# RMSNorm with a matmul on one core: two of the output stores divided by rows

## The chip, the core and the metric

The kernel runs on one core of a Trainium2 chip. The metric is the device time of one launch in microseconds, the median of several runs. A profile of one further run shows what every engine did: TensorE (PE, with weight loads as PEld), VectorE (DVE), ScalarE (ACT), GpSimd (POOL), SyncE (SP), and the DMA engines that move data between HBM and the on-chip buffer.

## What is computed

```python
def setup_inputs():
    batch, seq, dim, out_dim = 16, 1024, 512, 768
    return {
        "x": np.random.randn(batch, seq, dim).astype(np.float32),
        "gamma": np.ones(dim, dtype=np.float32),
        "weight": np.random.randn(dim, out_dim).astype(np.float32) * 0.1,
        "eps": np.float32(1e-5),
    }

def reference(x, gamma, weight, eps):
    rms = np.sqrt(np.mean(x ** 2, axis=-1, keepdims=True) + eps)
    x_norm = x / rms * gamma
    return np.matmul(x_norm, weight).astype(np.float32)
```

There are 16 × 1024 = 16,384 tokens. x has 512 and the output 768 float32 values for each, so 33.6 MB come in and 50.3 MB go out, and 1.6 MB of weights come in once.

## The kernel before

The tokens are handled as 128 tiles of 128 tokens. Each tile is cast to bf16, transposed (by TensorE, for some tiles by VectorE), multiplied with the weights, and scaled by 1/rms on its way from PSUM to an output buffer. ScalarE and VectorE take turns at that last step.

Transfers cover several tiles. The tokens of a group of 16 tiles lie so over the partitions that each partition holds 16 consecutive tokens; a store of 8 tiles is thus 128 rows of 8 × 768 × 4 = 24,576 consecutive bytes.

```python
XG, OG = 16, 8          # tiles of an input and of an output group
last = NT // OG - 1
x_first, x_size = stretches(XG, {0: [2, 2, 4, 8], **{g: [8, 8] for g in range(1, NT // XG)}})
o_first, o_size = stretches(OG, {0: [2, 2, 4], 1: [4, 4], last - 1: [4, 4], last: [4, 2, 2]})

def rows(ap, i, n):
    base, t = (x_first[i], x_size[i]) if i < XG else (i - i % XG, XG)
    return ap[base * P:(base + t) * P, :].rearrange("(p t) d -> p t d", t=t)[:, i - base:i - base + n, :]
...
xt = [sb(f"xt{n}", [P, XG, D], F32) for n in range(2)]     # two input buffers of 16 tiles
ot = [sb(f"ot{n}", [P, OG, O], F32) for n in range(3)]     # three output buffers of 8 tiles
```

The scaled tile goes into one of the three `ot` buffers. When the last tile of a stretch is in, SyncE issues the store of the stretch:

```python
def store(i):
    first, n = o_first[i], o_size[i]
    s = first // OG % 3
    if i == first + n - 1:
        src = ot[s][:, first % OG:first % OG + n, :]
        order.transfer(SP, lambda: SP.dma_start(out=rows(out, first, n), in_=src), reads=cells("ot", s, first % OG, n))
...
def finish_tile(i, a, engine):
    s = i // OG % 3
    before = [("ot", s, i % OG - 1)] if i == o_first[i] + o_size[i] - 1 else []
    scale(engine, ot[s][:, i % OG, :], ops[a][:, :O], rstd[:, i:i + 1],
          [("ops", a, 0), ("ops", a, 1), ("rstd", i)] + before, [("ot", s, i % OG)])
    store(i)
```

`order` keeps all instructions with the buffer cells that they read and write, and from these sets the semaphore waits: a tile is written into `ot` again only when the store that reads its former content has landed. The PSUM accumulators (`ops`) are three as well. The loads of x stand in the same SyncE queue as the stores:

```python
def load_until(i):
    while starts and starts[0] < i:
        load(starts.pop(0))
...
for j in range(1, NP):                       # pairs of tiles
    load_until((2 * j + AHEAD + XG - 1) // XG * XG)
    ...
    for i, engine in ((2 * j, ACT), (2 * j + 1, DVE)):
        a = accumulator()
        matmuls(i, a, range(K), feed)
        finish_tile(i, a, engine)
```

Of the kernel before, what the change touches and what calls it, by code (L numbers as in the profile page):

```python
# [16 lines left out]
P = 128  # L17
# [83 lines left out]
def kernel(  # L101
# [9 lines left out]
    PE, DVE, ACT, POOL, SP = nc.tensor, nc.vector, nc.scalar, nc.gpsimd, nc.sync  # L111
    order = Order(tc)
# [5 lines left out]
    out = out.flatten_outer_dims()  # L118
# [5 lines left out]
    XG, OG = 16, 8  # L124
    AHEAD = 20

    def stretches(group, parts):
        first, size, i = {}, {}, 0
        for g in range(NT // group):
            for n in parts.get(g, [group]):  # L130
                for t in range(i, i + n):
                    first[t], size[t] = i, n
                i += n
        return first, size

    last = NT // OG - 1
    x_first, x_size = stretches(XG, {0: [2, 2, 4, 8], **{g: [8, 8] for g in range(1, NT // XG)}})
    o_first, o_size = stretches(OG, {0: [2, 2, 4], 1: [4, 4], last - 1: [4, 4], last: [4, 2, 2]})

    def rows(ap, i, n):  # L140
        base, t = (x_first[i], x_size[i]) if i < XG else (i - i % XG, XG)
        return ap[base * P:(base + t) * P, :].rearrange("(p t) d -> p t d", t=t)[:, i - base:i - base + n, :]

    def sb(name, shape, dtype):
        return nc.alloc_sbuf_tensor(name, shape, dtype).ap()
# [14 lines left out]
    ot = [sb(f"ot{n}", [P, OG, O], F32) for n in range(3)]  # L160
# [7 lines left out]
    def cells(name, slot, i, n=1):  # L168
        return [(name, slot, t) for t in range(i, i + n)]
# [117 lines left out]
    def store(i):  # L287
        first, n = o_first[i], o_size[i]
        s = first // OG % 3
        if i == first + n - 1:  # L290
            src = ot[s][:, first % OG:first % OG + n, :]
            order.transfer(SP, lambda: SP.dma_start(out=rows(out, first, n), in_=src), reads=cells("ot", s, first % OG, n))

    def hold(lhsT, cell):
        run(PE, lambda: PE.ldweights(lhsT), [cell])  # L295
# [20 lines left out]
# [7 lines that stand above are left out]
# [157 lines left out]
```

## Time and profile before

| what | value |
|---|---|
| time, median of 3 runs | 209.54 us (209.4 to 209.75) |
| span of the profiled run | 207.7 us, granted TensorE clock 0.986 |
| DMA packets | 6064, 85.62 MB |
| stores of 8 tiles | 12, each 3072 KB, median 17.8 us from issue to landing |
| loads of 8 tiles | 15, each 2048 KB, median 21.6 us from issue to landing |
| store of tiles 40 to 47 | issued at 82.61 us, landed at 103.64 us |
| store of tiles 72 to 79 | issued at 129.45 us, landed at 153.15 us |

The span counts from the first to the last instruction of the core. The profile gives the busy time of each engine, a row of digits in which each stands for the busy tenths of one fortieth of the span, and the waits: engine and line, the thing waited for, microseconds in total, how many times, the longest. The DMA row is the mean over 16 DMA engines. A transfer from SyncE is divided over these engines, and it has landed when the last of its completion events is in.

### The profile page before, as it was taken

To read this page: it belongs to the slowest core of one execution; us is meant where nothing else is said; L and a number is where in the kernel's file an instruction comes from. 1 tells how busy PE (TensorE), PEld (TensorE's weight loads), DVE (VectorE), ACT (ScalarE), POOL (GpSimd) and SP (SyncE) were. 2 spreads that over 40 slices of the span, in tenths; PEclk is the share of its full clock that TensorE was granted. 3 is DMA by queue.
4 is the path that set the end of the run, shared out by engine and by line. 5 is a ranking of instruction groups with operands and counts; after the bars stand their busy time and mean duration, and the time that the engine had idled before them with its cause. 6 is when DMAs were issued, how large, how long until landed. Compare 5 with 4: busy or idle time off the path is not lost.

```text
span 207.7 us, 2772 instructions
## 1 busy us (share of the span) xinstructions
PE 193.6 (93%) x1212; PEld 72.9 (35%) x717; DVE 149.4 (72%) x255; ACT 144.5 (70%) x343; POOL 60.0 (29%) x34
## 2 busy tenths in 40 slices
PE   7889999999999999999999999999999999999900
PEld 1234444433344334333443333343434334433300
DVE  0455647998589957998589966998589966999310
ACT  4698897877768686877768686868778397863300
POOL 3147652047202740055200660006700175000000
PEclk9999999999999999999999999999999999999995
DMA  6999999999999999999999999999999999999992
GB/s 237 421 443 426 353 393 428 436 432 427 443 410 429 437 439 420 429 417 434 439 420 424 421 451 429 410 429 420 439 426 418 431 443 434 431 431 407 431 399 103
DMA packets 6064, 85.62 MB, mean 412 GB/s; under 512 B 674, under 2 KB 676, under 8 KB 1700
## 3 DMA queue, kind: packets, MB, share of 16 engines
q1 hardware_dynamic: 6048, 85.46, 97.4%
q8 instruction: 7, 0.11, 0.2%
q14 instruction: 5, 0.04, 0.0%
q10 hardware_dynamic: 4, 0.00, 0.0%
HBM read 35.13 MB, written 50.33 MB: 411 GB/s over the span
## 4 chain that ended last, share of the span: by engine, by line
PE 88%; DMA 4%; issue 1%; SPq 1%; POOL 1%; DVE 0%
PE ps L299 78%; PE ps L229 10%; DMA xt<-in_x_dram 4%; POOL xb L187 1%; DVE ot L280 0%; SPq L344 0%; SPq L176 0%; SPq L475 0%; SPq L434 0%
## 5 line engine op out<-in xcount | busy, mean ns | idle before, releaser
L299 PE MATMUL ps<-w_bf,xT 128*128 128x256 bf16 (+1 forms) x783 | 145.0, 325 | 1.3 <-DVE w_bf L280 0.2
L278 ACT ACTIVATE ot<-ps,rstd 128x768 f32<-128x768 f32 x64 | 57.5, 898 | 44.2 <-PE ps L299 39.6
L195 ACT ACTIVATE jk<-xt 128x512 bf16<-128x512 f32 x128 | 78.8, 619 | 5.0 <-DMA xt<-in_x_dram 4.9
L187 POOL CAST xb<-xt 128x2048 bf16<-128x2048 f32 (+3 forms) x21 | 46.4, 2218 | 113.0 <-DMA xt<-in_x_dram 110.1
L280 DVE TENSOR_SCALAR ot<-ps,rstd 128x768 f32<-128x768 f32 x64 | 64.8, 1013 | 8.6 <-PE ps L299 7.9
L295 PEld LDWEIGHTS <-xT 128*128 128x128 bf16 x400 | 39.3, 98 | 59.4 <-issue 51.5
L229 PE MATMUL ps<-ident_f,xb 128*128 128x128 f32 x200 | 54.4, 277 | 0.9 <-POOL xb L187 0.9
L238 DVE COPY xT<-ps 128x1024 bf16<-128x1024 bf16 (+1 forms) x53 | 34.6, 653 | 24.8 <-PE ps L229 23.1
L270 DVE STREAM_TRANSPOSE xTq<-xq 32x256 f32<-32x256 f32 x112 | 48.8, 435 | 3.4
L229 PEld LDWEIGHTS ps<-ident_f,xb 128*128 128x128 f32 x200 | 28.5, 143 | 46.3 <-issue 42.9
L299 PE MATMUL ps<-w_bf,xTq 128*128 128x256 bf16 (+1 forms) x217 | 41.8, 324 | 0.4
L195 ACT ACTIVATION_READ_ACCUMULATOR jk<-xt 128x1 f32 x128 | 24.4, 190 | 0.0
L295 PEld LDWEIGHTS <-xTq 128*128 128x128 bf16 x112 | 10.9, 98 | 14.5 <-issue 14.5
L259 POOL CAST xq<-xt 128x2048 bf16<-128x2048 f32 x7 | 13.2, 1893 | 0.0
L202 DVE RECIPROCAL rstd<-rms 128x8 f32<-128x8 f32 (+3 forms) x20 | 3.9, 193 | 7.4 <-ACT rms L200 7.2
L200 ACT ACTIVATE rms<-ssq,eps_sb 128x8 f32<-128x8 f32 (+3 forms) x20 | 6.0, 300 | 0.7
L299 PE MATMUL ps<-warm 128*128 128x512 bf16 x10 | 4.8, 629 | 1.4 <-DVE eps_sb L353 1.4
L278 ACT ACTIVATE w_bf<-w_f,g_sb 128x768 bf16<-128x768 f32 x2 | 1.9, 936 | 1.5 <-DMA w_f<-in_weight_dram 1.5
L376 DVE COPY g_sb<-ps 128x4 f32<-128x4 f32 x1 | 0.2, 163 | 3.2 <-PE ps L370 3.2
L340 ACT ACT_TABLE_LOAD x1 | 1.3, 1283 | 1.5 <-SPq L434 1.5
L280 DVE TENSOR_SCALAR w_bf<-w_f,g_sb 128x512 bf16<-128x512 f32 (+2 forms) x3 | 1.4, 482 | 0.9 <-DMA w_f<-in_weight_dram 0.9
L370 PEld LDWEIGHTS ps<-ident_f,g_row 2*128 2x128 f32 x2 | 0.3, 201 | 2.6 <-issue 2.6
(10 smaller groups left out, 2.0 us busy)
## 6 DMA issues: line engine op xcount, KB each, us to landing
out_dram<-ot SPq DMA_DIRECT2D x12, 3072.0 KB, 17.8
xt<-in_x_dram SPq DMA_DIRECT2D x15, 2048.0 KB, 21.6
out_dram<-ot SPq DMA_DIRECT2D x6, 1536.0 KB, 11.8
out_dram<-ot SPq DMA_DIRECT2D x4, 768.0 KB, 8.8
w_f<-in_weight_dram SPq DMA_DIRECT2D x2, 768.0 KB, 5.5
xt<-in_x_dram SPq DMA_DIRECT2D x2, 512.0 KB, 5.2
xt<-in_x_dram SPq DMA_DIRECT2D x1, 1024.0 KB, 9.2
g_row<-in_gamma_dram ACTq DMA_DIRECT2D x1, 2.0 KB
```

The source lines that it names most:

```text
L187: run(POOL, lambda: POOL.tensor_copy(out=xb[s][:, i % 8:i % 8 + n, :], in_=src), of, cells("xb", s, i % 8, n))
L195: run(ACT, lambda: ACT.activation(out=jk[j], in_=src[:, 0, :], func=AF.Square, accum_out=ssq[:, i:i + 1]), of, [("jk", j), ("ssq", i)])
L200: run(ACT, lambda: ACT.activation(out=rms[:, s], in_=ssq[:, s], func=AF.Sqrt, scale=1.0 / D, bias=eps_sb), [("ssq", t) for t in range(i, i ...
L202: run(DVE, lambda: DVE.reciprocal(out=rstd[:, s], in_=rms[:, s]), [("rms", i)], [("rstd", t) for t in range(i, i + n)])
L229: run(PE, lambda: PE.transpose(out=tp[b][:, t, h, :], in_=words[:, lo:lo + P], identity=ident_f), cells("xb", s, j % 4 * 2 + t) + ["ident" ...
L238: run(DVE, lambda: DVE.tensor_copy(out=dst[:, t:t + n, :], in_=src[:, t:t + n, :]), [("tp", b)], cells("xT", j % 4, t, n))
L259: run(POOL, lambda: POOL.tensor_copy(out=xq[s], in_=src), of, [("xq", s)])
L270: run(DVE, lambda: DVE.transpose(out=dst, in_=src), [("xq", s)], [("xTq", s)])
L278: run(ACT, lambda: ACT.mul(out=dst, in_=src, mul=r), reads, writes)
L280: run(DVE, lambda: DVE.tensor_single_scalar(out=dst, in_=src, scalar=r, op=mybir.AluOpType.mult), reads, writes)
L295: run(PE, lambda: PE.ldweights(lhsT), [cell])
L299: run(PE, lambda: PE.add_instruction(mybir.InstMatmult(name=nc.get_next_instruction_name(), engine=mybir.EngineType.PE, ins=[PE.lower_ap(r ...
```

## The change

The store of tiles 40 to 47 becomes two transfers, of the partitions 0 to 63 and 64 to 127. That of tiles 72 to 79 becomes two as well, of the partitions 0 to 119 and 120 to 127. All other stores stay in one piece. The same bytes go to the same places. Dividing a transfer by partitions changes how its rows are spread over the DMA engines; the purpose is another distribution of the rows of these two stores over the engines.

```diff
     o_first, o_size = stretches(OG, {0: [2, 2, 4], 1: [4, 4], last - 1: [4, 4], last: [4, 2, 2]})
+    o_rows = {40: [(0, 64), (64, P)], 72: [(0, 120), (120, P)]}
@@
         if i == first + n - 1:
             src = ot[s][:, first % OG:first % OG + n, :]
-            order.transfer(SP, lambda: SP.dma_start(out=rows(out, first, n), in_=src), reads=cells("ot", s, first % OG, n))
+            for lo, hi in o_rows.get(first, [(0, P)]):
+                order.transfer(SP, lambda lo=lo, hi=hi: SP.dma_start(out=rows(out, first, n)[lo:hi], in_=src[lo:hi]),
+                               reads=cells("ot", s, first % OG, n))
```

## The prediction

> **What bounds the kernel now.** I read the page first: the busy line and the forty slices, to see which unit is never idle.
>
> ```profile
> PE 193.6 (93%) x1212; PEld 72.9 (35%) x717; DVE 149.4 (72%) x255; ACT 144.5 (70%) x343; POOL 60.0 (29%) x34
> ...
> PE   7889999999999999999999999999999999999900
> ...
> DMA  6999999999999999999999999999999999999992
> ...
> q1 hardware_dynamic: 6048, 85.46, 97.4%
> ```
>
> Two rows of nines run side by side. TensorE works until the last two slices; the DMA row goes on to the end. Which of them sets the end is seen from the stages at the end (busy time of PE, PEld, DVE, ACT, POOL, then granted clock, DMA share, GB/s):
>
> ```profile
> 80.00:100.00 20.00, 19.90 (x130) 7.46 (x74) 17.44 (x30) 15.21 (x37) 7.17 (x3) 1.00 1.01 430
> 195.00:200.00 5.00, 2.61 (x17) 0.69 (x7) 2.04 (x2) 0.90 (x1) 0.00 (x0) 1.00 1.00 424
> 200.00:203.00 3.00, 0.00 (x0) 0.00 (x0) 0.00 (x0) 0.00 (x0) 0.00 (x0) 0.81 0.85 354
> 203.00:205.00 2.00, 0.00 (x0) 0.00 (x0) 0.00 (x0) 0.00 (x0) 0.00 (x0) 0.50 0.39 163
> 205.00:208.00 3.00, 0.00 (x0) 0.00 (x0) 0.00 (x0) 0.00 (x0) 0.00 (x0) 0.50 0.05 23
> ```
>
> In the middle the DMA engines are full (1.01). After 200 us no compute engine works at all and the transfers still run, with a share that falls 0.85, 0.39, 0.05: some of the sixteen are done early, a few late. The waits show the same end from the issuing side, and who else waits for stores:
>
> ```profile
> SPq L475 <- DMA out_dram<-ot: 7.4, 1, 7.4
> ...
> ACT ot L278 <- DMA out_dram<-ot: 2.9, 2, 1.9
> ```
>
> The 7.4 us is the tail after the last store is issued (198.96). The 2.9 us is ScalarE, which may not write a tile into one of the three `ot` buffers until the store of its former content has landed. One of its two cases is the buffer of the second divided store, tiles 72 to 79 (idle time in brackets):
>
> ```profile
> 153.23 0.90 ACT L278 ACTIVATE ot<-ps,rstd 128x768 f32<-128x768 f32 x1 [1.08 <-DMA out_dram<-ot]
> ```
>
> Last I took the completion events of the transfers from the trace, sixteen for each 128-row transfer, one from each engine's share. The last store's come at 202.19 for the first engine, the last four at 205.38, 205.59, 206.61 and 206.78. So the sixteen engines each work through their own list, the quickest is 4.6 us ahead of the slowest at the end, and the span (207.7) ends with the slowest. The trace does not number them.
>
> So the bound is the list of the slowest DMA engine. Anything that lengthens this one's work appears at the end in full; another engine has up to 4.6 us in hand. TensorE, which ends at 197.65, has about 6 us in hand by the last backlog.
>
> **What the Trainium skill says.** (1) "DMA: Bandwidth & Descriptors", section on why a DMA increments its semaphore by 16: a transfer from the Sync queue is spread over the largest number of engines up to 16 that divides the slowest dimension of both sides. The trace before agrees as far as it goes: sixteen events for every 128-row transfer. By this rule 64 rows use 16 engines with 4 rows each, 120 rows use 15 with 8 each, 8 rows use 8 with one each, on the lowest-numbered ones; no run shows these yet. (2) Same page, "Latency and other measured facts": engines 7 and 15 are usually the slower ones. Two engines do end last here, 0.17 us apart; which they are is not shown. (3) "SBUF — State Buffer", section "Door 1: The DMA port swizzle": partitions 0 to 63 reach only eight of sixteen ports, and a 1 MiB transfer on 64 partitions was measured at 196 GB/s against 328 on 128; (4) the same page, on hitting both halves with two DMAs: two at once, one per half, gave only 6% more than one. All transfers of the kernel before but the tiny one of gamma have 128 partitions, so its trace neither supports nor denies (3) and (4).
>
> **The change part by part.** It removes nothing and adds no bytes. It adds two DMA issues on SP, at some 0.34 us each (332/343/348 ns, minimum, median and maximum of the 22 stores); SP waits 108 us in total for VectorE alone, so these are free. The instruction order shows one more semaphore for ScalarE and VectorE when they reuse the buffers of the two stores, no other movement.
>
> *64 and 64 rows.* In the trace an engine's share of this store, 8 rows of 24 KB, takes 7.28 us (first completion of the load ahead at 92.82, of the store at 100.10): 0.91 us a row. With 4 rows from each half the bytes of an engine stay the same. If ports are not shared the cost is zero. If two engines share a port as (3) says, 4 rows take up to 7.28 instead of 3.64 us. Two engines that are d apart overlap for 3.64 − d in each half, so each loses 2 × (3.64 − d). Ten of the sixteen pass the load ahead within 0.57 us (92.82 to 93.39); with d about 0.3 they lose 6.7 us. The slowest, at 96.31, is 3.5 us behind the first and 1.1 behind its nearest, so it loses between 0.3 and 5.0. At the end the quick ones have 4.6 in hand: 6.7 − 4.6 = 2.1 us late. A pair in the middle, which has about 2.1 in hand, would be 4.6 late. Estimate, from the trace and this page: 2 to 4.6 us, if sharing is real.
>
> *120 and 8 rows.* One engine loses 8 rows, 7.3 us. Eight engines get one row more, 0.9 us. The rest keep theirs. The relief counts only if that engine is the slowest, and then only up to the next one: 206.78 − 206.61 = 0.17 us. If a slow one is among the eight, as engine 7 would be, the end moves by about +0.9 − 0.17 to +0.9. Port sharing again comes on top: if consecutive blocks of 8 rows go to one engine, such a block lies over two ports, and most of the fifteen share both with another; the 8-row piece lies on two ports for eight engines. Engines in step would lose up to 6.7 us once more, and now with nothing in hand; after the first division they are less in step with some, so I take 3 to 6.7.
>
> *Stores that land later.* The store of tiles 40 to 47 lands at 103.64, and its buffer is written again at 106.23: 2.6 us to spare. That of tiles 72 to 79 lands at 153.15 and has none. A delay goes on to ScalarE, and by the three accumulators to TensorE, but these wait beside a DMA list that is still full, so I add nothing for them.
>
> Sums: without sharing, −0.2 to +0.9, so 209.4 to 210.4. With sharing in the halves alone: 2 to 4.6 plus up to 0.9, so 211.5 to 215. With sharing in both: 2.1 + (3 to 6.7) + 0.9, so +6 to +9.7, 215.5 to 219.2.
>
> **The rivals.** *A: balance only.* Ports do not matter to engines that are out of step anyway, and the new division merely moves 8 rows from one engine. For it: the spread of 3.5 us at 96 us, nearly the 3.64 us of a half; a small gain is what such uneven rows would be meant for. Against: ten engines are within 0.57 us. It makes 209.4 to 210.4. *B: halves share ports, and the margin of the quick engines hides most of it.* 211.5 to 215. *C: both stores pay.* For it: (3) and (4) and the full DMA row, which leaves no idle time to hide in. Against: which rows an engine gets of 120 is not known to me. It makes about 217.5. *D: TensorE becomes the bound*, because the late landings hold its buffers: TensorE would have to lose more than the 6 us of backlog, possible only within C.
>
> **Range and chances.** I give A 0.45, B 0.25, C and D 0.30. The middle of this weight lies in the lower part of B: 212.5 us. The range 208.5 to 219.5 takes in A with a little gain by another order of the engines, and nearly all of C. Two per cent is 4.2 us: slower begins at 213.7, which is C, D and about half of B: 0.42. Faster by 2% would mean 205.3, a gain of 4.2 us where even the quickest engine ends only 4.6 before the slowest: 0.03. The rest, 0.55, is within 2%.
>
> **What would show it.** Completion events of the halves: sixteen each; if sharing is real, the quick engines need about 14 us for the 64 and 64 rows instead of 7.3, and the packets of 24,576 bytes take well over their usual time there. If A holds they take 7.3. The 120-row piece has 15 events and the 8-row one 8, else the engine count is wrong. The tail after the last compute should still be DMA alone. The prediction is wrong if the slowest engine catches up by more than 0.2 us without a cost to the others, or if TensorE shows new waits that outlast the DMA backlog.

## The result and the profile after

The kernel with divided stores takes 221.66 us (median of 4 runs, 220.84 to 222.34), the kernel before beside it 209.64 us. The ratio is 1.057, 95% interval 1.054 to 1.061: 12.0 us slower, beyond the upper end of the predicted range (219.5).

The page of the changed kernel, first the busy line, then the forty slices of TensorE, of the DMA engines and of the rate:

```profile
PE 197.0 (89%) x1212; PEld 73.3 (33%) x717; DVE 149.8 (68%) x255; ACT 143.7 (65%) x343; POOL 60.0 (27%) x34
...
PE   7799999999999999999879799998958999999910
...
DMA  6999999999999999999999999999989999999993
GB/s 237 428 433 428 338 429 440 428 414 442 420 428 440 431 424 420 443 315 222 361 369 393 420 431 425 421 443 344 242 333 393 406 399 424 420 422 397 411 403 131
...
q1 hardware_dynamic: 6071, 85.46, 97.1%
```

The bytes are the same 85.46 MB, and the DMA row is still nines. But the GB/s row has two holes, 315 222 361 and 344 242 333. A DMA engine that is busy and moves half is not idle: its packets last longer. One slice is 5.5 us, so the holes lie at about 94 to 110 and 149 to 165 us, where the two divided stores are carried out. The stages say it more sharply, the same three stretches in the kernel before and in the changed one (last three columns: granted clock, DMA share, GB/s):

```profile
85.00:92.00 7.00, 7.00 (x48) 2.81 (x28) 6.67 (x13) 4.62 (x12) 1.38 (x1) 1.00 1.01 433
95.00:102.00 7.00, 6.95 (x46) 2.50 (x25) 4.75 (x10) 6.12 (x15) 3.73 (x2) 1.00 1.02 437
102.00:109.00 7.00, 6.95 (x47) 2.79 (x28) 5.37 (x9) 4.51 (x12) 0.00 (x0) 1.00 0.99 424
```

```profile
85.00:92.00 7.00, 7.00 (x48) 2.91 (x29) 6.67 (x13) 4.75 (x12) 1.17 (x1) 1.00 1.02 435
95.00:102.00 7.00, 6.95 (x45) 2.46 (x25) 4.77 (x9) 6.12 (x16) 3.73 (x2) 1.00 1.05 255
102.00:109.00 7.00, 6.95 (x46) 2.84 (x28) 4.36 (x7) 2.27 (x7) 0.00 (x0) 1.00 0.92 302
```

Ahead of the store of tiles 40 to 47 the two are alike, 433 and 435 GB/s. In it 437 becomes 255 at a full DMA share. TensorE (6.95 of 7.00 in both) notices nothing yet. The waits of the changed kernel show what follows:

```profile
ACT ot L279 <- DMA out_dram<-ot: 10.8, 3, 6.7
...
PE ps L302 <- ACT ot L279: 8.4, 5, 3.7
DVE ot L281 <- DMA out_dram<-ot: 6.7, 2, 3.9
```

ScalarE and VectorE wait for buffers whose stores land late (2.9 us of this before, for ScalarE alone), and TensorE waits for ScalarE. Yet the end is again DMA alone:

```profile
205.00:212.00 7.00, 4.83 (x30) 1.37 (x14) 2.77 (x3) 1.80 (x2) 0.00 (x0) 1.00 0.97 411
212.00:215.00 3.00, 0.00 (x0) 0.00 (x0) 0.00 (x0) 0.00 (x0) 0.00 (x0) 0.84 0.92 387
215.00:220.00 5.00, 0.00 (x0) 0.00 (x0) 0.00 (x0) 0.00 (x0) 0.00 (x0) 0.50 0.31 129
```

The completion events date the loss. Below are the last event of a transfer (slowest engine) in both kernels, and how much later it is:

| last event of | before | changed | later |
|---|---|---|---|
| load ahead of the store of tiles 40 to 47 | 96.31 | 95.58 | −0.7 |
| store of tiles 40 to 47 | 103.64 | 110.75 | 7.1 |
| load ahead of the store of tiles 72 to 79 | 145.83 | 153.15 | 7.3 |
| store of tiles 72 to 79 | 153.15 | 165.23 | 12.1 |
| store of tiles 80 to 87 | 160.41 | 172.50 | 12.1 |
| last store | 206.78 | 219.37 | 12.6 |

There are two steps, one at each divided store, and next to nothing between and after them. Nothing is won back.

The packets tell the same. Of the 1536 packets of 24,576 bytes none took over 1.5 us in the kernel before (usual: 0.912). In the changed kernel 124 did, the longest 5.61. The time above 0.912 is 85.0 us in sum around the first store and 77.9 around the second. Load packets of 16,384 bytes took 29 us in sum above what they took before, just behind the two stores. All this is (85.0 − 0.8 + 77.9 − 1.1 + 29.2) / 16 = 11.9 us as a mean over the sixteen engines, nearly all of the 12.6 us by which the profiled run is longer.

### The profile page after: what moved, and what is told of

Read it like the earlier page. It is cut to its first block, busy times and chain, and to the rows that moved or that the text cites. A ratio compares the mean times of both kernels' runs of the same rounds, so it can differ in the third digit from the quotient of the medians.

```text
span 220.3 us, 2774 instructions
## 1 busy us (share of the span) xinstructions
PE 197.0 (89%) x1212; PEld 73.3 (33%) x717; DVE 149.8 (68%) x255; ACT 143.7 (65%) x343; POOL 60.0 (27%) x34
## 3 DMA queue, kind: packets, MB, share of 16 engines
q1 hardware_dynamic: 6071, 85.46, 97.1%
## 4 chain that ended last, share of the span: by engine, by line
PE 50%; DMA 30%; DVE 10%; issue 2%; ACT 2%; SPq 1%; POOL 0%; ACTq 0%
PE ps L302 44%; DMA xt<-in_x_dram 30%; PE ps L230 6%; DVE ot L281 4%; DVE xTq L271 3%; DVE xT L239 2%; ACT jk L196 1%; ACT ot L279 1%; POOL xb L188 0%; SPq L347 0%; SPq L177 0%; SPq L294 0%; DVE rstd L203 0%; ACTq L93 0%; SPq L478 0%
## 5 line engine op out<-in xcount | busy, mean ns | idle before, releaser
L302 PE MATMUL ps<-w_bf,xT 128*128 128x256 bf16 (+1 forms) x783 | 148.8, 329 | 10.3 <-ACT ot L279 8.4
L188 POOL CAST xb<-xt 128x2048 bf16<-128x2048 f32 (+3 forms) x21 | 46.4, 2218 | 125.8 <-DMA xt<-in_x_dram 125.8
```

Of the source, the lines that this page charges most:

```text
L188: run(POOL, lambda: POOL.tensor_copy(out=xb[s][:, i % 8:i % 8 + n, :], in_=src), of, cells("xb", s, i % 8, n))
L302: run(PE, lambda: PE.add_instruction(mybir.InstMatmult(name=nc.get_next_instruction_name(), engine=mybir.EngineType.PE, ins=[PE.lower_ap(r ...
```

## The experiments

Three theories: P, engines that read rows behind the same port of the on-chip buffer slow each other; M, only the number of rows that an engine gets counts; T, each added transfer costs the same. Which rows lie behind which port, P takes from the page under (3) in the prediction, "SBUF — State Buffer", section "Door 1: The DMA port swizzle": four consecutive rows share a port, rows 0 to 31 lie behind eight ports, 32 to 63 behind the same eight, and 64 to 127 behind the other eight in the same way. That the rows of a piece go to its engines in consecutive blocks, and that the engines of a whole store share no port, is assumed; the trace does not number the engines. All edits are to the changed kernel. Times stand beside the kernel before on the same chip (209.5 to 209.7).

### One division at a time

```diff
-    o_rows = {40: [(0, 64), (64, P)], 72: [(0, 120), (120, P)]}
+    o_rows = {40: [(0, 64), (64, P)]}                 # halves only
+    o_rows = {72: [(0, 120), (120, P)]}               # 120 and 8 only
```

> Only the store of tiles 40 to 47 is divided, into 64 and 64 rows. Theory P (engines that read rows behind the same port slow each other): in the changed kernel the packets of this store took about 5 us longer per engine, of which the quick engines have 4.6 us in hand and TensorE's waits add some: 213 to 216 us. Theory M (only the number of rows per engine counts; that is unchanged, 4 and 4): 209.6 us, no change. Theory T (each added transfer with its semaphore costs the same, whatever its rows): half of the 12 us, about 215.6 us.

> Only the store of tiles 72 to 79 is divided, into 120 and 8 rows. Theory P: packets slow here as in the changed kernel, about 5 us per engine and more on those with the 8-row piece: 214 to 217 us. Theory M: 209.4 to 210.5 us (one row more on eight engines, eight fewer on one). Theory T: about 215.6 us.

Halves only: 215.56 us, ratio 1.027 (1.024 to 1.030). 120 and 8 only: 217.03 us, ratio 1.035 (1.033 to 1.037). The costs, 5.9 and 7.3 us, make 13.2 together, against 12.0 for both. The extra packet time is 82.7 us around the first store in the one run and 83.8 around the second in the other, as in the changed kernel. Both halves of the change cost; M is refuted, P and T not yet separated.

### The same number of transfers, all rows in each

```diff
-    o_rows = {40: [(0, 64), (64, P)], 72: [(0, 120), (120, P)]}
+    o_rows = {40: [(0, 4), (4, 8)], 72: [(0, 4), (4, 8)]}     # tiles now
...
-            for lo, hi in o_rows.get(first, [(0, P)]):
-                ... out=rows(out, first, n)[lo:hi], in_=src[lo:hi] ...
+            for lo, hi in o_rows.get(first, [(0, n)]):
+                ... out=rows(out, first, n)[:, lo:hi], in_=src[:, lo:hi] ...
```

> Both stores are divided, but by tiles: 4 and 4 tiles, each with all 128 rows of 12 KB. The number of transfers, of semaphores and of waits is that of the changed kernel. Theory P and theory M: no change, 209.2 to 210.2 us, and packets of 12 KB at their usual 0.46 us. Theory T: about 221 us.

209.85 us, ratio 1.0007 (0.9997 to 1.0018), and no 24 KB packet over 1.5 us. Its list of transfers:

```profile
out_dram<-ot SPq DMA_DIRECT2D x10, 3072.0 KB, 16.1
out_dram<-ot SPq DMA_DIRECT2D x10, 1536.0 KB, 15.1
```

Ten whole stores of 8 tiles are left and ten of half the size, as many transfers as in the changed kernel. Issues, semaphores and smaller packets cost nothing that can be measured. T falls: it is which rows a transfer has.

### The same bytes and rows for each engine, other ports

```diff
-    o_rows = {40: [(0, 64), (64, P)], 72: [(0, 120), (120, P)]}
+    o_rows = {40: [(0, 64)]}        # rows 64 to 127 of these tiles are not stored
+    o_rows = {40: [(32, 96)]}       # rows 0 to 31 and 96 to 127 are not stored
```

> Of tiles 40 to 47 only the rows 0 to 63 are stored; rows 64 to 127 are left out. Every DMA engine then has 4 rows, 3.6 us, less than in the kernel before. Theory P: the sixteen engines read through eight ports, so packets take about 1.8 us instead of 0.91 and the saving is lost: 208 to 212 us. Theory M (rows per engine alone): 206 us, packets at 0.91 us.

> Of tiles 40 to 47 only the rows 32 to 95 are stored; the others are left out. Same bytes, same 4 rows for every engine as in the run with the rows 0 to 63; only the ports differ, one for each engine. Theory P: packets at their usual 0.91 us, 206 us. Theory M: also 206 us, as for the rows 0 to 63. The pair decides: P wants a difference of 2 us or more, M none.

Rows 0 to 63: 209.45 us, ratio 0.9996 (0.998 to 1.001). Rows 32 to 95: 206.72 us, ratio 0.987 (0.985 to 0.988). Both leave out 1.57 MB, 4 rows or 3.6 us for each engine; the first gains nothing by it, the second 2.8 us. The stretch 95 to 102 us and the one after it, with rows 0 to 63 and then with rows 32 to 95:

```profile
95.00:102.00 7.00, 6.95 (x46) 2.51 (x25) 4.74 (x10) 6.13 (x15) 3.74 (x2) 1.00 0.97 297
102.00:109.00 7.00, 6.95 (x47) 2.80 (x28) 5.37 (x9) 4.50 (x12) 0.00 (x0) 1.00 0.96 372
```

```profile
95.00:102.00 7.00, 6.95 (x46) 2.50 (x25) 4.74 (x9) 6.13 (x15) 3.74 (x2) 1.00 1.04 438
102.00:109.00 7.00, 6.95 (x47) 2.74 (x27) 5.37 (x9) 4.57 (x12) 0.00 (x0) 1.00 0.95 380
```

Every column for the compute engines agrees to within 0.1 us; the rate differs, 297 against 438 GB/s. Extra time of the store packets: 39.7 us against 9.3. Which rows the transfer has decides it, as P wants. The rows' places in HBM move along with the partitions, and no run separates the two. But a cause on the HBM side would have to make 0 to 63 and 64 to 127 slow and 32 to 95 between them fast, which the map of the ports gives by itself.

### Fewer shared rows

```diff
-    o_rows = {40: [(0, 64), (64, P)], 72: [(0, 120), (120, P)]}
+    o_rows = {40: [(32, 96), (0, 32), (96, P)]}
```

> The store of tiles 40 to 47 in three pieces: rows 32 to 95, then 0 to 31, then 96 to 127. If 4 consecutive rows go to each engine, the middle 64 rows give each of sixteen engines a port of its own; in the 32-row pieces two engines share one. Theory P: the middle piece runs at full speed (0.91 us a packet), sharing is left in half of the bytes, 3.6 us at most, which the 4.6 us in hand of the quick engines cover: 209.6 to 212 us. Theory M: 209.6 us. Theory T (three transfers): more than the kernel with two halves, 218 us.

213.62 us, ratio 1.019 (1.014 to 1.025). The middle piece runs at full speed: its first engine needs 3.66 us (93.08 to 96.74), its last 4.00. The two outer pieces do not, and the extra packet time is 33.5 us against 82.7 with two halves. Fewer shared rows, less loss, as P wants, and T falls again (three transfers, yet cheaper than two). The time is 1.6 us above what I expected: I had let the 4.6 us in hand of the quick engines pay for it, and the slowest engine itself lost 4.2 (95.59 to 107.10, 7.3 before).

### The two pieces of tiles 72 to 79

```diff
-    o_rows = {40: [(0, 64), (64, P)], 72: [(0, 120), (120, P)]}
+    o_rows = {72: [(0, 120)]}       # the last 8 rows of these tiles are not stored
+    o_rows = {72: [(120, P)]}       # the first 120 rows are not stored
```

> Of tiles 72 to 79 only the rows 0 to 119 are stored; the last 8 are left out. If the 120-row piece is what costs in the 120 and 8 rows (blocks of 8 consecutive rows lie over two ports), the time stays near that of both pieces, 213 to 216 us, with packets of 1.5 to 2 us; the packets of 3 us and more should be gone, if they belong to the 8-row piece. If the 8-row piece is what costs, 209 to 210 us.

> Of tiles 72 to 79 only the rows 120 to 127 are stored; the other 120 are left out. Theory P: eight engines read one row each, four of them through one port: packets of up to 3.6 us. Most of the store's 7.3 us per engine is gone, so the DMA backlog at the end is small: 202 to 206 us. Theory M: the eight packets take 0.91 us; 202 to 203 us.

120 rows alone: 214.19 us, ratio 1.023 (1.019 to 1.027). 8 rows alone: 205.02 us, ratio 0.978 (0.977 to 0.980). So the 120 rows bring 4.6 of the 7.3 us and the 8 rows about 2.7 on top. The longest packet falls from 5.93 us to 3.50 without the 8 rows. The 120 rows also speak against a limit per half of the buffer: 64 of them lie in one half and 56 in the other, and still they cost 4.6 us.

With the 8 rows alone the time tells little. All sixteen engines finish the last store between 201.94 and 202.14, 3.2 to 3.4 us after its issue at 198.71, so in that run compute is the bound. The packets do not show what I expected of P: the four that start together (140.89 to 141.13) take 0.912 us each. That the 8 rows cost something is seen only behind the 120.

### One store later

```diff
-    o_rows = {40: [(0, 64), (64, P)], 72: [(0, 120), (120, P)]}
+    o_rows = {48: [(0, 64), (64, P)]}
```

> The 64 and 64 rows one store later, at tiles 48 to 55. In the queue this store is followed by two loads, not by another store as that of tiles 40 to 47 is. If the slowest engine lost so much at 40 to 47 because the engines ahead of it were already reading their own rows for the next store through its port, it loses less here, as loads write: 211 to 214 us. If only the two engines of a port within the same store matter, it is as at tiles 40 to 47: 215 to 216 us.

215.07 us, ratio 1.026 (1.024 to 1.028): the time is that of the halves at tiles 40 to 47, and the expectation for the time is missed. The packets agree with it all the same. At tiles 40 to 47, with a store behind, six packets take more than 2.2 us, up to 3.93; here, with loads behind, none is over 2.13, which fits two to a port (twice 0.912 is 1.82) and no more. From the last event of the load or store ahead to its own last event the store takes 12.8 us (102.91 to 115.72), not 15.4 (95.35 to 110.78). In these two profiled runs the slowest engine thus loses 2.6 us less in the store and 0.9 more in the first load behind (6.5 against 5.6), and its last event comes 1.8 earlier (212.07 against 213.86). The medians differ by only 0.5, with intervals that overlap; the profiled run with the division at tiles 40 to 47 (216.75) is the slowest of its four.

### Smaller pieces

```diff
-    o_rows = {40: [(0, 64), (64, P)], 72: [(0, 120), (120, P)]}
+    o_rows = {40: [(r, r + 16) for r in range(0, P, 16)]}
+    o_rows = {40: [(r, r + 32) for r in range(0, P, 32)]}
```

> The store of tiles 40 to 47 in eight pieces of 16 rows, one row for each engine in each piece. Theory P: sixteen rows lie behind four ports, so four engines share one and the 7.3 us of an engine become up to 29: 222 to 236 us, with packets of 3 to 4 us. Theory H (not the port counts but the half of the buffer, 64 partitions, which carries half of the rate): as with 64 and 64 rows, 215 us, packets of 1.8 us.

> The store of tiles 40 to 47 in four pieces of 32 rows, two rows for each engine in each. 32 rows lie behind eight ports, as 64 do. Theory P and theory H: as with 64 and 64 rows, 213 to 217 us. If the number of pieces mattered, it would be between that and the run with pieces of 16.

Pieces of 16: 221.9 us, ratio 1.058 (1.051 to 1.066), over 220.47 and 223.39; the other two of its four runs are in a slower state, over 1.5% above the fastest, and the profile is of one of them. Pieces of 32: 217.81 us, ratio 1.039 (1.035 to 1.043). With 16 rows, behind four ports, the loss is 12.3 us, just below the range that P gave (222 to 236). Pieces of 32 cost 8.2 us, 2.3 more than halves (5.9) on as many ports, so the number of pieces matters too once they share. The times 5.9, 8.2 and 12.3 alone would therefore not rule out a limit per half of the buffer (theory H). The packets speak for four to a port: over 2.2 us take 6 with halves, 7 with pieces of 32 and 31 with pieces of 16. What speaks most clearly against H is the 120 rows above.

## Why the prediction was wrong

**What bounds the kernel: right.** The end is the list of the slowest DMA engine, and the changed kernel ends the same way, with its tail of DMA alone.

**Number of engines for each piece: right.** The 120-row transfer has fifteen events that come with data and the 8-row one eight. The missing one and eight are given at once: the first event comes 0.5 us after the issue (135.61 after 135.07, 136.01 after 135.54). That is the Trainium skill's rule for engines and semaphore counts ("DMA: Bandwidth & Descriptors", the section on the increment by 16), and this trace agrees. By M alone this change would have been worth −0.2 to +0.9 us, as computed under A.

**The chances: wrong.** I gave A, no sharing, 0.45. The Trainium skill had it: "SBUF — State Buffer", section "Door 1: The DMA port swizzle", says that rows 0 to 63 reach only eight of sixteen ports. The pair of runs with 64 rows shows 297 against 438 GB/s with other rows. The note on engines 7 and 15, behind the +0.9, stays untested: the trace has no engine numbers.

**The step that failed** is "At the end the quick ones have 4.6 in hand: 6.7 − 4.6 = 2.1 us late", together with "it loses between 0.3 and 5.0" for the slowest. I took the slowest engine to be sheltered by being out of step with its partner. In the run with halves only the engine that ends last took at least 15.4 us for its 8 rows (every engine was through the load by 95.35, this one through its rows at 110.78) instead of 7.3, so it lost 8.1. The first engine to finish lost at most 3.2 (92.74 to 103.20, 10.46 instead of 7.28), where I had 6.7 for those in step. Being behind is no shelter. While an engine is still on its piece, those that have finished go on to the next store and read their own rows of it, so a late engine can meet two others at a port. Packets of 3.93 us with a store behind, and none over 2.13 with loads behind, fit this. So does the second half of the store: from the last event of the first half to its own it takes 10.7 us with a store behind (100.09 to 110.78) and 7.4 with loads behind (108.31 to 115.72), where two engines that share a port all the time need 7.3 for their four rows. Which engines meet the trace does not tell, so the meeting itself is argued and not shown.

So the margin of the quick engines did not count: the engine that had none lost the most. That the quickest engine of the changed kernel ends 12.3 us later (202.19 to 214.46) does not contradict this. It ends 3.2 us after the last store is issued in both kernels (198.96 and 211.24), so it waits for compute there.

**The sizes.** Halves: 2 to 4.6 us estimated, and only 2.1 in the sum for C, 5.9 measured. 120 and 8: 3.9 to 7.6 in that sum (sharing and the extra row), 7.3 measured. The 120 rows brought 4.6 of it, within the 3 to 6.7 that stood there; the 8 rows cost about 2.7 us in place of 0.9. Load packets behind each store, about 1.8 us per engine in all, stood in no sum.

**Rival D.** TensorE did get waits (8.4 us for ScalarE), but they did not become the bound: the slowest engine's list goes on without a break. From the store of tiles 80 to 87 on, its completions are as far apart as before (172.50 to 219.37 is 46.9 us, 160.41 to 206.78 is 46.4). TensorE had less in hand than the 6 us of the prediction: with the 8 rows alone, where compute is the bound, the last store lands at 202.14, only 4.6 before 206.78. In the changed kernel compute falls back by 12.3 us and SyncE still waits 7.7 us for the last store (7.4 before), because compute falls back along with the slowest engine: a load has landed only when the last engine is through its share, and the longest wait of GpSimd for one grew from 15.7 to 24.6 us.

## What to carry to other kernels

Where DMA is the bound, divide a store by tiles, not by partitions: here the same number of transfers cost nothing by tiles (ratio 1.0007) and 5.7% by rows. A row division can keep every engine's byte count equal and still cut its rate (437 to 255 GB/s here), so ask which partitions are read at the same time; 64 rows across the middle (32 to 95) ran at full rate. Look for it where the DMA share stays at 1.0 and GB/s falls, and do not credit the slowest engine with the slack of the others.

## What the runs showed beyond that

Two engines at a port do not slow each other from the first packet behind a load. With pieces of 32 behind a load the two packets of an engine in the first piece took 0.91 us each, or little more (1.88 us for both, as a mean over the engines), though two engines should share each port; in the second piece, from 94.18 on, packets of 1.8 us come. With the halves behind another store (tiles 48 to 55) packets of 1.2 and 1.3 us come at once and 1.9 within a microsecond. The 8 rows alone also come behind a load. That an engine reads ahead by some packets while its load is still being written could explain these three; no run here tests it. With four engines at a port it is otherwise: in the run with pieces of 16 the very first packets behind the load, at 92.27 and 92.29, took 2.0 us.

Load packets became slow behind the changed store also where ports were not shared: 14.3 us in sum between 105 and 125 us with the rows 32 to 95 alone, 2.3 in the kernel before. And in the runs with the rows 32 to 95 alone and with the 8 rows alone, nine store packets each took 1.5 to 1.8 us, nearly all of them the last ones of the next whole store (102.52 to 102.84 and 149.16 to 149.40), where theory P gives no sharing. The cause of both stays open.
